# Output projection of a two-layer trunk by seven half-size products, on one core

## The chip, the core and the metric

One core of a Trainium2 chip runs the whole program as one launch. The metric is the device time of the launch in microseconds (us), the median of the runs. The engines are PE (TensorE), DVE (VectorE), ACT (ScalarE), POOL (GpSimd) and SP (SyncE), which in this kernel only issues DMA transfers. Each engine works through its own queue in order and waits at an instruction until the semaphores that it names are there, so an instruction that waits holds up everything behind it on its engine.

## The reference

Two layers with D = 1024 channels and T = 1024 positions, then one RMSNorm. Each layer, cut to what matters here:

```
h = rmsnorm(x) * (1 + scale) + shift
p = h @ w_in                      # q, k, v and gates of 8 heads, 256 wide each
heads 0-3: y = sigmoid(o) * layernorm(mlstm(q, k, v)) * silu(z)
heads 4-7: y = layernorm(retention(rotary(q), rotary(k), v)) * silu(z)
x = x + gate * (concat(y) @ w_out)   # (1024 x 2048) @ (2048 x 1024)
```

The change concerns the last line. Everything is f32.

## The kernel before, in words

**Arithmetic on PE.** An f32 factor is split in two rounded parts, H (a cast, on ACT) and L (the value minus H, a subtraction on POOL or DVE; `split_to`, L589 to L591). `mm3` (L134 to L136) then makes each f32 product of three matmuls, H by H, H by L and L by H, summed in PSUM. The usual matmul has 128 rows and 512 columns. In the profile, a cast is the line L590, a POOL or DVE subtraction L591, and `b`, `wH`, `wL`, `raw`, `g`, `th`, `acc` are tags of SBUF buffers (62, 6, 6, 4, 6, 5 and 4 of them); a tag's buffer comes free when its last reader is done. `pp` and `pa` are four PSUM banks each.

**Order.** PE's queue is written by hand: the main line runs a generator of "units" of 12 matmuls of 512 columns (`run_units`), and after each unit `tick` lets the generators that were started with `launch` do a step, so that attention, norms and loads lie between the units of a projection. ACT, DVE, POOL and SP are ordered by a scheduler from the program's data flow, except in the first stretch, which is written out. All DMA transfers go through SP's queue.

**A head.** For each of the eight heads, `gate_path` makes the gates g (stored to DRAM as `gdr`, L523), then q, k and v come with their own projections, k's rows through DRAM (`kdr`: stored by L622, loaded by `k_rows`, L632, scaled by ACT at L646 and split by DVE at L648), and `launch(attention(...))` puts the head's attention beside the projections of the next head. Its norm is a chain over engines: DVE statistics (L808, L809), DVE `va` (L824), POOL power (L825), DVE `nmu` (L827), ACT `n` (L830); the result goes to DRAM as `ndr` (L842).

**Output projection.** `out_units` runs four passes, 2 halves of 512 positions by 2 halves of 512 output channels (cc). Each pass goes over k = 16 pieces of 128 inner channels, and each piece is 4 tiles of 128 positions by one `mm3`: 2 x 2 x 16 x 4 x 3 = 768 matmuls of 128x512 in a layer. `OutLoads.stage` prepares a piece: it loads a 128x512 block of w_out and splits it (L590 on ACT, L591 on DVE for cc = 0 and on POOL for cc = 1); for cc = 0 it also loads `ndr` and `gdr`, multiplies them (L882, DVE), casts the product times the norm's gain (L885, ACT) and makes the low part (L886, DVE, a product and a subtraction in one). The split y is kept in `b` for cc = 1. After the 16 pieces `out_evac` multiplies each bank by the adaLN gate (L927), adds the residual (L928) and squares it for the next norm (L931). At the end of layer 0 `norm_later` normalizes, transposes on PE (L296) and splits h for layer 1 (L1076 and about); `first` starts the gates' projections from it while the second half is made. At the very end `final_rows` does the closing norm tile by tile.

Of the kernel before, what the change touches and what calls it, by code (L numbers as in the profile page):

```python
# [11 lines left out]
F32 = mybir.dt.float32  # L12
# [57 lines left out]
def tile_hybrid_trunk(ctx, tc, x, c, positions, w_ada, b_ada, norm_g, w_in, conv_w, conv_b,  # L70
# [62 lines left out]
    def mm3(o, lt, rt, start, stop):  # L133
        PE.matmul(o, lt[0], rt[0], start=start, stop=False)  # L134
        PE.matmul(o, lt[0], rt[1], start=False, stop=False)  # L135
        PE.matmul(o, lt[1], rt[0], start=False, stop=stop)  # L136
# [21 lines left out]
    mdr = [dpool.tile([NH, T], F32, name=f"mdr{l}") for l in range(DEPTH)]  # L158

# [552 lines left out]
    def attention(l, hg, gt, qT, kT, kt, vs, gp, rot):  # L712
# [120 lines left out]
        def finish(j):  # L833
# [10 lines left out]
            if hg == 3 and j == NCH - 1:  # L844
                with tc.issue_after(last.ins):
                    load_rotary(rot)

# [17 lines left out]
    class OutLoads:  # L865
        def __init__(self, l):
            self.l, self.yT, self.ready = l, [None] * 16, []
            self.todo = [(half, cc, k) for half in range(2) for cc in range(2) for k in range(16)]

        def stage(self, n=1):  # L870
            for half, cc, k in self.todo[:n]:
                raw = wt("raw", 512, 4)
                Q.dma_start(raw, w_out[self.l, k * P:(k + 1) * P, cc * 512:(cc + 1) * 512])
                wH, wL = wt("wH", 512, 6, F32R), wt("wL", 512, 6, F32R)
                split_to((wH, wL), raw, G if cc else V)
                if cc == 0:
                    hg, ct = k // 2, k % 2
                    yr, gr = wt("g", 512, 6), wt("g", 512, 6)
                    Q.dma_start(yr, ndr[self.l][hg][half].rearrange("b j t -> (b j) t")[ct * P:(ct + 1) * P])
                    Q.dma_start(gr, gdr[self.l][hg][ct][half])  # L880
                    g4 = gr.rearrange("p (a b c) -> p a b c", a=4, c=32)
                    V.tensor_tensor(g4, yr.rearrange("p (b a c) -> p a b c", a=4, c=32), g4, ALU.mult)  # L882
                    y2 = (bt(F32R), bt(F32R))
                    gn = gn_col(self.l, hg, ct)
                    A.activation(y2[0], gr, AF.Copy, scale=gn)  # L885
                    V.scalar_tensor_tensor(y2[1], gr, gn, f(y2[0]), ALU.mult, ALU.subtract)  # L886
                    self.yT[k] = y2
                self.ready.append((self.yT[k], (wH, wL)))
            del self.todo[:n]
# [5 lines left out]
    def out_units(l, half, cc, loads, gb, xnew, ss, done=None):  # L895
        banks = [ps_a() if cc else ps_p() for _ in range(4)]

        def product(k, piece, tt):
            (yH, yL), w = piece
            ts = slice(tt * P, (tt + 1) * P)  # L900
            mm3(banks[tt], (yH[:, ts], yL[:, ts]), w, k == 0, k == 15)

        together = 12 if done else 16
        for k in range(together):
            piece = loads.take()
            for tt in range(4):
                product(k, piece, tt)
            yield
        if not done:
            out_evac(l, half, cc, banks, gb, xnew, ss, range(4))  # L910
        else:
            pieces = [loads.take() for _ in range(together, 16)]
            for tt in range(4):
                for k in range(together, 16):
                    product(k, pieces[k - together], tt)
                out_evac(l, half, cc, banks, gb, xnew, ss, (tt,))
                done((tt,))
                yield

    def out_evac(l, half, cc, banks, gb, xnew, ss, rows):  # L920
        for tt in rows:
            row = half * 4 + tt
            xr = bt()
            srcx = x[row * P:(row + 1) * P] if l == 0 else xdr[row]
            Q.dma_start(xr, srcx[:, cc * 512:(cc + 1) * 512])
            tmp = wt("th", 512, 5)
            V.tensor_tensor(tmp, banks[tt], gb[cc], ALU.mult)  # L927
            V.tensor_tensor(xr, xr, tmp, ALU.add)  # L928
            if l < DEPTH - 1:
                Q.dma_start(xdr[row][:, cc * 512:(cc + 1) * 512], xr)  # L930
            A.activation(tmp, xr, AF.Square, accum_out=ss[:, tt, cc:cc + 1])  # L931
            xnew[tt][cc] = xr
# [13 lines left out]
    def norm_later(l, xt, ss, hT, half):  # L946
        sst = row_rstd(ss, "nrm")
        norm_scale(xt, sst)
# [14 lines left out]
    def final_rows(xn, ss, half, fg, rows):  # L963
        sst = row_rstd(ss, "nrm", rows)
        for tt in rows:
            V.tensor_tensor(xn[tt][1], xn[tt][1], fg[1], ALU.mult)
# [12 lines left out]
    def gains_later(xn, fg):  # L979
        for tt in range(4):  # L980
            yield 2
            V.tensor_tensor(xn[tt][0], xn[tt][0], fg[0], ALU.mult)
# [58 lines left out]
    for l in range(DEPTH):  # L1041
# [85 lines left out]
        for hg in range(8):  # L1127
# [3 lines left out]
            if hg > 0:  # L1131
                gp = [[None, None], [None, None]]
                run_units(gate_path(l, hg, hT, gp, 0, 1 if hg == 7 else 2))
# [16 lines left out]
            if hg == 7:  # L1150
                loads = OutLoads(l)
# [3 lines left out]
            if hg == 1 and l == 0:  # L1155
                launch(rotary_tables(), 0)
            if hg == 5:
# [3 lines left out]
        nhT = [[None, None] for _ in range(KT)]  # L1161
        if l == DEPTH - 1:
            fg = []
# [4 lines left out]
        for half in range(2):  # L1168
# [43 lines left out]
```

## Time and profile before

| what | value |
|---|---|
| median of 3 runs | 2354.23 us (2353.19 to 2355.81) |
| profiled execution: its span, from its first to its last instruction | 2353.8 us, granted clock 0.994 |
| PE busy | 2307.7 us (98%), 12597 matmuls recorded |
| DVE, ACT, POOL busy | 1289.8, 893.3 and 882.8 us (55, 38 and 38%) |
| DMA | 260.50 MB, 111 GB/s over the span |
| output projection of layer 0 | about 1016 to 1205 us |
| output projection of layer 1 | about 2160 to 2344 us, then the closing norm until 2353.8 |

The profiled execution's own time stands beside the median as 2353.8 to 2354.23 us. Busy PE is the union of matmuls that overlap in the pipeline: one 128x512 matmul is recorded with some 0.39 us, while the next starts 0.23 us later, so what a matmul costs is read from start to start.

### The profile page before, as it was taken

What the parts mean: (1) busy time and instruction counts of PE and PEld (TensorE: products, weight loads), DVE (VectorE), ACT (ScalarE), POOL (GpSimd) and SP (SyncE); (2) the same over time, 40 slices, a digit from 0 to 9 for tenths busy, and PEclk for the clock granted to TensorE, in tenths of its full rate; (3) what the DMA queues carried; (4) which work ended last, traced back from release to release, by engine and by line L of the source; (5) the groups of instructions that cost most, each with busy time, mean ns of one, the idle gap of its engine ahead of it and who ended that gap; (6) DMA issues with size and microseconds to landing.
All of it is one profiled execution on the core that took longest, in us unless ns stands there. A gap on an engine that the chain in (4) does not pass through costs nothing.

```text
span 2353.8 us, 34446 instructions
## 1 busy us (share of the span) xinstructions
PE 2307.7 (98%) x12597; PEld 1982.2 (84%) x12597; DVE 1289.8 (55%) x2699; ACT 893.3 (38%) x1736; POOL 882.8 (38%) x841
## 2 busy tenths in 40 slices
PE   5999999999999999999999999999999999999998
PEld 4888888988978988988888888888898888888886
DVE  7375687656454445475525655454543444555753
ACT  5535443444332322343434444344443322224442
POOL 0344333443244343323453444343334434341313
PEclk8999999999999999999999999999999999999999
DMA  7223232434332433277422333322323242425762
GB/s 243 74 68 99 73 88 72 116 94 126 108 99 71 117 83 102 81 241 254 167 78 77 82 76 78 80 68 76 81 70 86 77 112 77 117 82 159 266 231 77
DMA packets 326971, 260.50 MB, mean 111 GB/s; under 512 B 75893, under 2 KB 262013, under 8 KB 326801
## 3 DMA queue, kind: packets, MB, share of 16 engines
q1 hardware_dynamic: 326800, 258.30, 37.4%
q8 instruction: 99, 1.62, 0.3%
q14 instruction: 72, 0.58, 0.1%
HBM read 202.61 MB, written 55.61 MB: 110 GB/s over the span
## 4 chain that ended last, share of the span: by engine, by line
PE 93%; DVE 2%; DMA 2%; issue 1%; POOL 1%; ACT 1%; SPq 1%; POOLq 0%; ACTq 0%; DVEq 0%
PE pp L134 24%; PE pp L136 24%; PE pp L135 24%; PE pa L136 6%; PE pa L134 6%; PE pa L135 6%; PE pa L742 1%; DMA b<-in_w_ada_dram 1%; DMA b<-in_x_dram 1%; PE pa L296 0%; DVE b L233 0%; DMA dm<-mdr 0%; POOL wL L591 0%; SPq L995 0%; POOL b L591 0%
## 5 line engine op out<-in xcount | busy, mean ns | idle before, releaser
L134 PE MATMUL pp<-b,wH 128*128 128x512 f32 x1792 | 712.7, 398 | 1.1 <-ACT b L1073 1.1
L135 PE MATMUL pp<-b,wH 128*128 128x512 f32 x1792 | 708.2, 395 | 1.3 <-DVE b L1076 1.3
L136 PE MATMUL pp<-b,wL 128*128 128x512 f32 x1792 | 708.2, 395 | 0.0
L591 POOL TENSOR_TENSOR wL<-raw,wH 128x512 fp32r<-128x512 f32 x338 | 449.2, 1336 | 578.5 <-ACT wH L590 506.5
L136 PEld LDWEIGHTS pp<-b,wL 128*128 128x128 f32 x1792 | 337.8, 189 | 81.0
L134 PEld LDWEIGHTS pp<-b,wH 128*128 128x128 f32 x1792 | 338.7, 189 | 74.1 <-issue 1.5
L135 PEld LDWEIGHTS pp<-b,wH 128*128 128x128 f32 x1792 | 338.4, 189 | 73.7 <-DVE b L1076 2.0
L590 ACT CAST wH<-raw 128x512 fp32r<-128x512 f32 x402 | 247.3, 617 | 390.4 <-PE pp L135 138.3
L136 PE MATMUL pp<-wH,b 128*128 128x256 f32 (+1 forms) x1152 | 353.0, 306 | 1.2 <-DVE b L886 1.1
L134 PE MATMUL pp<-wH,b 128*128 128x256 f32 (+1 forms) x1152 | 353.6, 307 | 0.0
L135 PE MATMUL pp<-wL,b 128*128 128x256 f32 (+1 forms) x1152 | 352.6, 306 | 0.0
L591 POOL TENSOR_TENSOR b<-acc,b 128x256 fp32r<-128x256 f32 (+1 forms) x208 | 200.4, 983 | 319.9 <-ACT b L590 306.0
L136 PEld LDWEIGHTS pp<-wH,b 128*128 128x128 f32 x1152 | 217.2, 189 | 13.5 <-DVE b L886 2.0
L134 PEld LDWEIGHTS pp<-wH,b 128*128 128x128 f32 x1152 | 216.9, 188 | 10.7
L135 PEld LDWEIGHTS pp<-wL,b 128*128 128x128 f32 x1152 | 216.6, 188 | 10.6
L590 ACT CAST b<-acc 128x256 fp32r<-128x256 f32 (+1 forms) x208 | 93.6, 487 | 201.5 <-DVE acc L685 136.5
L608 DVE SCALAR_TENSOR_TENSOR acc<-pp,cols,acc 128x511 f32<-128x511 f32 (+2 forms) x192 | 142.7, 743 | 44.2 <-ACT acc L603 42.0
L591 POOL TENSOR_TENSOR sL<-th,sH 128x384 fp32r<-128x384 f32 x64 | 69.5, 1086 | 155.4 <-ACT sH L590 141.2
L134 PE MATMUL pa<-wH,b 128*128 128x512 f32 x256 | 101.1, 395 | 0.0
L135 PE MATMUL pa<-wL,b 128*128 128x512 f32 x256 | 100.9, 394 | 0.0
L136 PE MATMUL pa<-wH,b 128*128 128x512 f32 x256 | 100.7, 393 | 0.0
L612 ACT ACTIVATE th<-acc 128x512 f32<-128x512 f32 x64 | 40.4, 632 | 146.6 <-DVE acc L610 79.8
(237 smaller groups left out, 3470.9 us busy)
## 6 DMA issues: line engine op xcount, KB each, us to landing
raw<-in_w_in_dram SPq DMA_DIRECT2D x274, 256.0 KB
raw<-in_w_out_dram SPq DMA_DIRECT2D x128, 256.0 KB
b<-in_w_ada_dram SPq DMA_DIRECT2D x96, 256.0 KB
gdr<-g SPq DMA_DIRECT2D x64, 256.0 KB
ndr<-zt SPq DMA_DIRECT2D x128, 128.0 KB
g<-ndr SPq DMA_DIRECT2D x64, 256.0 KB
g<-gdr SPq DMA_DIRECT2D x64, 256.0 KB
acc<-kdr SPq DMA_DIRECT2D x192, 64.0 KB
```

The source lines that it names most:

```text
L134: PE.matmul(o, lt[0], rt[0], start=start, stop=False)
L135: PE.matmul(o, lt[0], rt[1], start=False, stop=False)
L136: PE.matmul(o, lt[1], rt[0], start=False, stop=stop)
L590: A.copy(dst[0], src)
L591: eng.tensor_tensor(dst[1], src, f(dst[0]), ALU.subtract)
L608: V.scalar_tensor_tensor(acc[:, d:], pt[:, 0:HALF - d], wcol, acc[:, d:], ALU.mult, ALU.add)
L612: A.activation(th, acc, AF.Tanh, scale=0.5)
L742: PE.matmul(pd, kk[i][:, jo + P:jo + CH], qd, start=dt == 0 and i == 0, stop=dt == 1 and i == 1)
```

## The change

**Seven products instead of eight.** The layer's product is Y (1024 x 2048) times W (2048 x 1024). Both are cut into quarters (positions x inner channels, inner x output channels), and the four result quarters come from seven products of quarters in Strassen's scheme (Winograd's form), in the order 1, 2, 5, 6, 3, 7, 4. Each product has 8 pieces of 12 matmuls: 7 x 8 x 12 = 672 matmuls in a layer. PE's row count goes from 12511 to 12319.

- Products 1 and 2 take quarters of Y and W as they are, product 3 a sum of Y's quarters and a quarter of W, products 5, 6 and 7 sums of W's quarters, with sums of Y's quarters (5, 6) or a quarter (7), and product 4 a quarter of Y and a sum of W's. The sums of Y are made on DVE in `OutPrep.stage` (`add`, L939 after the change), the split of y and of sums on ACT and DVE (L595, L596), all splits of weights on POOL.
- Four times in a layer a product is added to a bank that must first be saved or used: after product 1 the banks are copied to `acc` by ACT (L1037), after 5 to buffers of other tags (L1037), after 6 to `g` (L1053, and added to the first copy on DVE, L1054), after 7 to `th`.
- `bases` adds the copies, times the gate, to the residual rows ahead of the last products (L1005, L1006).
- Each product ends with its last 2 pieces in the order of the tiles (the very last product with 4).

**What runs earlier.** `weight_sums`, launched after head 3, loads the 32 blocks of w_out in a layer, makes 32 differences on DVE (L894) and stores them to DRAM (`tdr`). `gated_later`, launched as each half of heads 0 to 6 is normalized, loads `ndr` and `gdr`, multiplies (DVE), scales by the gain (ACT) and stores the gated output to DRAM (`ydr`): 28 of them in a layer, 256 KB each. The output projection loads `ydr` and `tdr`. Head 7 is gated inside the output projection, as all heads were before.

**Head 7.** Both units of its gate path come after q, k and v, beside its attention; before, one of them came first.

**Norm at the layer's end.** The eight scalings alternate between DVE and ACT.

**Scheduler.** It is told to order by its own simulated timeline (`schedule_with_timeline_sim=True`). So ACT, DVE, POOL and SP have another order in many places of the whole body, except in the hand-written start.

The diff, cut to its core (lines in [] are shortened):

```diff
+    def gated(l, hg, ct, half, out=None):
+        yr, gr = wt("g", 512, 6), wt("g", 512, 6)
+        Q.dma_start(yr, ndr[l][hg][half].rearrange("b j t -> (b j) t")[ct * P:(ct + 1) * P])
+        Q.dma_start(gr, gdr[l][hg][ct][half])
...
+        V.tensor_tensor(o4, yr.rearrange("p (b a c) -> p a b c", a=4, c=32), g4, ALU.mult)
+        A.activation(out, out, AF.Copy, scale=gn_col(l, hg, ct))
+    def gated_later(l, hg, half):
+        for ct in range(2):
+            Q.dma_start(ydr[l][2 * hg + ct][half], gated(l, hg, ct, half))
+            yield 2
+    def weight_sums(l):
...
+        for i in range(KT):
+            w11, w12 = load(i, 0), load(i, 1)
+            yield 2
+            difference(w11, w12, w11, 1, i)
...
+        ORDER = (1, 2, 5, 6, 3, 7, 4)
         def stage(self, n=1):
+            for p, i in self.todo[:n]:
+                if p == 1:
+                    self.y11[i] = src = self.y(i, 0)
+                elif p == 2:
+                    self.y12[i] = src = self.y(8 + i, 0)
+                    self.y21[i] = self.y(i, 1)
+                elif p == 5:
+                    self.y22[i] = self.y(8 + i, 1)
+                    src = self.add(V, self.y21[i], self.y21[i], self.y22[i], ALU.add)
+                elif p == 6:
+                    self.s2[i] = src = self.add(V, bt(), self.y22[i], self.y11[i], sub)
+                elif p == 3:
+                    src = self.add(V, self.y12[i], self.y12[i], self.s2[i], sub)
+                else:
+                    src = self.y11[i] if p == 7 else self.y22[i]
+                y2 = self.split_y(src, V)
+                if p == 2:
+                    self.add(V, self.y11[i], self.y11[i], self.y21[i], sub)
...
+    def out_projection(l, prep, gb, fg, nhT):
+        def save(banks, res, place):
+            def evac(tt):
+                res[tt] = wt("acc", 512, 4) if place is None else spare(place + tt)
+                A.copy(res[tt], banks[tt])
...
+        run_units(out_units(prep, b1, True, False, save(b1, c1, None)))
...
+        run_units(out_units(prep, b2, True, False, save(b2, c5, 0)))
...
-                run_units(gate_path(l, hg, hT, gp, 0, 1 if hg == 7 else 2))
+                if hg < 7:
+                    run_units(gate_path(l, hg, hT, gp))
...
-    with tile.TileContext(nc) as tc:
+    with tile.TileContext(nc, schedule_with_timeline_sim=True) as tc:
```

**Three places in the order.** The names are tags with a number for the use.

First, ACT at the start of head 4's attention in layer 0. L830 (L835 after the change) is the norm `n` of the attention, L646 (L651) scales head 4's k rows. Before:

```order
522 L830 ACTIVATE n_7337<-pa_7314,nmu_7335,rsd_7332 128x256
523 L830 ACTIVATE n_7337<-pa_7318,nmu_7335,rsd_7332 128x256
524 L590 CAST wH_7702<-raw_7700 128x512
525 L518 ACTIVATE th_7352<-pp_7301 128x512
526 L646 ACTIVATE b_7200<-acc_7142 128x512
527 L646 ACTIVATE b_7205<-acc_7147 128x512
```

and after:

```order
535 L651 ACTIVATE b_7496<-acc_7436 128x512
536 L523 ACT_TABLE_LOAD
537 L523 ACTIVATE th_7571<-pp_7523 128x512
538 L651 ACTIVATE b_7501<-acc_7441 128x512
539 L595 CAST wH_8023<-raw_8021 128x512
540 L651 ACTIVATE b_7577<-acc_7506 128x512
541 L595 CAST sH_7597<-th_7593 128x384
542 L595 CAST wH_8029<-raw_8027 128x512
543 L523 ACTIVATE th_7656<-pp_7601 128x512
544 L835 ACTIVATE n_7641<-pa_7618,nmu_7639,rsd_7636 128x256
545 L835 ACTIVATE n_7641<-pa_7622,nmu_7639,rsd_7636 128x256
```

The k rows' scalings moved from behind the norm to ahead of it.

Second, DVE inside the output projection of layer 0. Before, two input pieces of the first pass (L882 gates, L886 low part of y, L591 low part of the weights):

```order
1307 L591 TENSOR_TENSOR wL_11016<-raw_11013,wH_11015 128x512
1308 L882 TENSOR_TENSOR g_11020<-g_11019,g_11020 128x512
1309 L882 TENSOR_TENSOR g_11085<-g_11084,g_11085 128x512
1310 L886 SCALAR_TENSOR_TENSOR b_11025<-g_11020,cols_388,b_11024 128x512
1311 L886 SCALAR_TENSOR_TENSOR b_11090<-g_11085,cols_388,b_11089 128x512
1312 L591 TENSOR_TENSOR wL_11081<-raw_11078,wH_11080 128x512
```

and after, two pieces of product 6, each with the subtraction that makes its y, the one that makes product 3's y from it, and the split's (L596):

```order
1386 L939 TENSOR_TENSOR b_11818<-b_11584,b_10902 128x512
1387 L939 TENSOR_TENSOR b_11297<-b_11297,b_11818 128x512
1388 L596 TENSOR_TENSOR b_11821<-b_11818,b_11820 128x512
1389 L939 TENSOR_TENSOR b_11842<-b_11609,b_10914 128x512
1390 L939 TENSOR_TENSOR b_11326<-b_11326,b_11842 128x512
1391 L596 TENSOR_TENSOR b_11845<-b_11842,b_11844 128x512
```

DVE's weight splits and gate products of the projection are gone from here, and sums of y stand there, every one with both inputs in SBUF.

Third, ACT inside the output projection. Before, its casts of weights (L590), the scaled cast of y (L885) and, between them, casts of the next layer's h (`b<-acc`):

```order
791 L885 ACTIVATE b_11817<-g_11813,cols_388 128x512
792 L590 CAST wH_11922<-raw_11920 128x512
793 L590 CAST b_11840<-acc_11838 128x512
794 L885 ACTIVATE b_11855<-g_11851,cols_388 128x512
795 L590 CAST wH_11960<-raw_11958 128x512
```

and after, where product 5 ends and product 6 begins on the same banks (`pa`):

```order
796 L595 CAST wH_11906<-raw_11904 128x512
797 L1037 COPY cf_11872<-pa_11679 128x512
798 L595 CAST b_11844<-b_11842 128x512
799 L1037 COPY n_11880<-pa_11680 128x512
800 L1037 COPY kw_11888<-pa_11681 128x512
801 L595 CAST b_11856<-b_11854 128x512
802 L595 CAST wH_11932<-raw_11930 128x512
803 L1037 COPY zt_11896<-pa_11682 128x512
```

The four copies stand between the casts of pieces that product 6 needs.

230 lines of the change are left out of this document (153 added, 77 removed).

## The prediction

> **What bounds the kernel now.** I read the windows by stage first, since the change takes work from one stage and puts work into the others (the two long rows are the heads of layers 0 and 1, the row behind each is that layer's output projection, the last row the closing norm).
>
> ```profile
> core 0: us, PE busy (x) PEld busy (x) DVE busy (x) ACT busy (x) POOL busy (x), PEclk, DMA share, GB/s
> 80.00:1010.00 930.00, 922.65 (x5231) 801.31 (x5230) 532.78 (x1185) 341.84 (x668) 363.33 (x346) 1.00 0.33 92
> 1010.00:1203.00 193.00, 191.86 (x897) 157.57 (x896) 105.62 (x161) 75.14 (x135) 70.88 (x53) 1.00 0.63 209
> 1220.00:2150.00 930.00, 929.26 (x5269) 807.98 (x5266) 473.15 (x1041) 348.44 (x686) 372.64 (x368) 1.00 0.31 82
> 2150.00:2345.00 195.00, 193.99 (x893) 159.03 (x891) 113.27 (x180) 76.66 (x141) 55.43 (x44) 1.00 0.60 203
> 2345.00:2354.00 9.00, 0.00 (x0) 0.00 (x0) 2.87 (x8) 2.06 (x4) 1.39 (x2) 0.69 0.38 145
> ```
>
> PE is busy for 99% or more of each stage but the last, at a granted clock (PEclk) of 1.00. Beside PE's own weight loads no engine is busy for more than 59% of any. So the time is the number of matmuls times their price from start to start. That price I took from PE's timeline, which has 40 matmuls of 128x512 without a gap from the first to the last of these rows:
>
> ```profile
> 1202.50 0.39 PE L136 MATMUL pa<-wH,b 128*128 128x512 f32 x1
> ...
> 1211.57 0.39 PE L136 MATMUL pp<-b,wL 128*128 128x512 f32 x1
> ```
>
> That is 39 steps in 9.07 us, 0.2326 us each; the 0.39 us are one matmul's own length in the pipeline. A piece of 12 matmuls takes 2.79 us.
>
> Then PE's waits, and the rows of its timeline at those that the change moves:
>
> ```profile
> PE pa L184 <- DMA rows<-in_b_ada_dram: 7.5, 1, 7.5
> PE pa L207 <- DMA rows<-in_c_dram: 2.9, 1, 2.9
> PE pa L134 <- ACT b L646: 2.7, 1, 2.7
> ```
>
> ```profile
> 689.61 0.58 PE L134 MATMUL pa<-b,b 128*128 128x256 f32 x1 [2.74 <-ACT b L646]
> 1017.44 0.50 PE L136 MATMUL pp<-wH,b 128*128 128x512 f32 x1 [1.14 <-DVE b L886]
> 1212.40 0.33 PE L296 MATMUL pa<-ident,b 128*128 128x128 f32 x1 [0.22 <-DVE b L291]
> 1213.19 0.33 PE L296 MATMUL pa<-ident,b 128*128 128x128 f32 x1 [0.46 <-DVE b L291]
> ```
>
> The two waits on DMA are in the start, which stays as it is. After it no DMA holds PE.
>
> **The change, part by part.**
>
> *Matmuls.* 768 - 672 = 96 fewer in a layer, 192 in all, every one 128x512: 192 x 0.2326 = 44.7 us, all on the path, since PE is the bound. The Trainium skill (TensorE: Matmul & The Clock Gate, "Wait — 56ns, not 53.3ns?") gives 215.7 ns from start to start for 512 columns in a warm array; by that the saving would be an estimated 41.4 us. The row here says 0.2326, and the sum goes by the row.
>
> *Waits that go.* At 689 us PE waits for L646 on ACT. ACT's and DVE's timelines show why:
>
> ```profile
> 684.82 1.19 DVE L824 TENSOR_TENSOR va<-mv,kc 128x2 f32<-128x2 f32 x1
> 687.02 1.02 ACT L830 ACTIVATE n<-pa,nmu,rsd 128x256 f32<-128x256 f32 x2 [2.86 <-DVE nmu L827]
> 687.93 0.61 ACT L590 CAST wH<-raw 128x512 fp32r<-128x512 f32 x1
> 688.44 0.60 ACT L518 ACTIVATE th<-pp 128x512 f32<-128x512 f32 x1
> 688.93 1.15 ACT L646 ACTIVATE b<-acc 128x512 fp32r<-128x512 f32 x2
> ```
>
> L646 stands in ACT's queue behind the attention's norm L830, which waits 2.86 us for DVE and POOL. In the new order the k rows' scalings stand nine and six rows ahead of that norm, so they run as soon as their loads land: -2.74 us. At 1017 us PE's first output piece waits for the low part of its y (L886), which goes through load, product, cast and low part in the projection itself; now the first product's y is gated long before and only split here: -1.14. At the layer boundary the last 2 pieces go tile by tile, so three tiles are evacuated before the last matmul, and the norm's chain begins earlier: -0.68. Together -4.6 us.
>
> *The tail.* The last 12 matmuls of a tile and the closing chain are of the same kinds as before; 0.
>
> *Bank copies.* Eight times (four in a layer) the next product adds to banks that ACT must first have copied. The copy itself isn't in the trace of before; its nearest row is an ACT operation of the same shape that reads PSUM, and beside it the cast that can stand ahead of it:
>
> ```profile
> L603 ACT ACTIVATE acc<-pp,cols 128x512 f32<-128x512 f32 x64 | 49.5, 773 | 23.7 <-PE pp L136 23.6
> L590 ACT CAST wH<-raw 128x512 fp32r<-128x512 f32 x402 | 247.3, 617 | 390.4 <-PE pp L135 138.3 <-PE pp L136 136.9 <-PE pa L136 58.0
> ```
>
> The last bank's product ends, and nine matmuls (tiles 0 to 2 of the next piece) lie before its reuse: 9 x 0.2326 = 2.09 us. One cast and the copy take 0.62 + 0.77 = 1.39, two casts and the copy 2.01: hidden, by 0.08 us at the least. If ACT's front cast waits for DVE (1.25 us, the stretched row below) with another cast behind it, the wait is 2.01 + 1.25 - 2.09 = 1.17 us. Ends 0 and 8 x 1.17 = 9.4 us; the copies are issued among casts that mostly have their data, so nearer the lower end, a quarter: +2.4.
>
> *DVE and POOL in the output projection.* Here lies the danger. DVE's and POOL's timelines, from before's projection:
>
> ```profile
> 1033.41 0.74 DVE L886 SCALAR_TENSOR_TENSOR b<-g,cols,b 128x512 fp32r<-128x512 f32 x1
> ...
> 1034.94 0.68 DVE L882 TENSOR_TENSOR g<-g,g 128x512 f32<-128x512 f32 x1
> 1035.54 0.68 DVE L591 TENSOR_TENSOR wL<-raw,wH 128x512 fp32r<-128x512 f32 x1
> 1036.41 1.25 DVE L886 SCALAR_TENSOR_TENSOR b<-g,cols,b 128x512 fp32r<-128x512 f32 x1 [0.19 <-ACT b L885]
> ```
>
> ```profile
> 1034.98 2.13 POOL L591 TENSOR_TENSOR sL<-th,sH 128x384 fp32r<-128x384 f32 x1 [3.91 <-ACT sH L590]
> ```
>
> POOL's subtraction has no overlap elsewhere and takes 1.03 us, and the 128x512 one 1.30:
>
> ```profile
> 683.72 1.02 POOL L591 TENSOR_TENSOR sL<-th,sH 128x384 fp32r<-128x384 f32 x1 [3.14 <-ACT sH L590]
> 684.70 1.30 POOL L591 TENSOR_TENSOR wL<-raw,wH 128x512 fp32r<-128x512 f32 x1
> ```
>
> Here POOL took 2.13 us and ended (1037.11) 0.89 after DVE's second operation (1036.22); the DVE operation that started meanwhile took 1.25 instead of 0.74 and ended (1037.66) 0.55 after POOL. So with both inputs in SBUF the two take turns: after a change of hands an operation costs the other's end plus 0.89 of 1.02 (0.13 less) or 0.55 of 0.74. In a row, DVE's start every 0.60 us. Per layer I count for 56 pieces: 60 POOL subtractions (56 weight splits, 4 in `bases`) and 140 two-input DVE operations (56 splits of y, 32 sums, 4 gate products, 24 in `bases`, 4 in `sum_up`, 20 in `out_rows`). With turns: 60 x (1.30 - 0.13) + 60 x 0.55 + 80 x 0.60 = 151 us. PE needs 56 x 2.79 = 156 us. That is 97%, and it just fits. With DVE's 0.60 throughout and POOL's 1.30 it is 162, with the full 0.68 173. Ends for a layer: 0 and 17 us; I take the row with turns, since these operations do alternate there, and 1 us a layer for a queue that is so full: +2.
>
> The Trainium skill (SBUF — State Buffer, "Who interferes with whom") states that GpSimd has DVE's second port pair, that a DVE instruction with two SBUF inputs contends with a GpSimd one that reads SBUF, and that the one that issues first has the pair for its whole instruction while the other "fully blocks". The rows agree that they block each other, with ends 0.55 and 0.89 us after the other's. By whole durations the sum would come out at the upper end, +17 us a layer: that is the first rival.
>
> *Layer 0's norm in product 7.* The first half's norm now has a whole product's time, but its 9 DVE operations run in that full queue. Ends: 0, and 9 x (1.25 - 0.68) = 5.1 us; most of it lies beside product 7's units, so +1.
>
> *Gated outputs and weight sums in the heads.* Per layer 28 gate products and 32 subtractions on DVE and 28 scalings on ACT come into the heads' stage. From the groups of before:
>
> ```profile
> L882 DVE TENSOR_TENSOR g<-g,g 128x512 f32<-128x512 f32 x64 | 61.6, 968 | 32.7 <-DMA g<-gdr 32.4 <-issue 0.2
> L885 ACT ACTIVATE b<-g,cols 128x512 fp32r<-128x512 f32 x64 | 45.8, 723 | 67.7 <-DVE g L882 67.6
> ```
>
> DVE goes from 533 to 533 + 60 x 0.97 = 591 of 930 us, ACT from 342 to 362: covered by idle time. Transfers: 56 loads, 28 stores, 32 loads and 32 stores of 0.262 MB are 39 MB, 42 GB/s on top of 92 at a share of 0.33, so about 0.48: covered. The stores wait for their data at the head of SP's queue, and weight loads stand behind them. What such a wait costs, SP's timeline shows:
>
> ```profile
> 682.13 7.98 SPq L523 DMA_DIRECT2D gdr<-g  x2
> 690.29 1.84 SPq L632 DMA_DIRECT2D acc<-kdr  x4
> 692.17 1.00 SPq L317 DMA_DIRECT2D raw<-in_w_in_dram  x2
> ```
>
> SP stood for 8 us and nothing of PE waited for the loads behind: 0 as long as the loads are that early.
>
> *The new order everywhere.* In the heads PE idled 930 - 922.65 = 7.35 us in layer 0 and 0.74 in layer 1. The order of four engines is another now. Ends: all of the rest gone, -(7.35 - 2.74 + 0.74) = -5.3; or layer 1 as bad as layer 0, +6.6. Nothing excludes either; added work speaks for the upper one: +2.5.
>
> Sum: 2353.8 - 44.7 - 4.6 + 2.4 + 2 + 1 + 2.5 = 2312.4 us for the profiled execution. The median of the runs is 0.4 above its span, so 2312.8; I say 2312.
>
> **The rivals.**
>
> *The shared lane becomes the bound* (the upper end above, 6 to 17 us a layer, so +12 to +34): about 2322 to 2344. For it: the 97%, no room in products 2, 5, 6 and 3 (two DVE operations and a split a piece, 1.30 + 1.36 = 2.66 of 2.79). Against it: product 1, 7 and 4 are lighter (1.98 a piece), and six weight buffers let the splits run ahead.
>
> *The order also removes the old waits*: layer 0's heads run like layer 1's, and the new costs are hidden: 2353.8 - 44.7 - 4.6 - (7.35 - 2.74 - 0.74) = 2300.6. For it: layer 1 shows that this body can run with 0.74. Against: layer 0 has the rotary tables and layer 1's adaLN columns besides.
>
> *Slower than before*: the same lane, if each operation pays its stretched time without the other gaining. Place: products 2, 5, 6 and 3, 64 pieces in two layers. It decides from 2.79 + 49.3 / 64 = 3.56 us a piece. With DVE at 1.25 twice and POOL at 2.13 a piece takes 4.63, 64 x 1.84 = 118 us more: 2422. Against it: the stretched times hold the other's turn, so the same time is counted twice.
>
> *The matmuls don't go*: PE's row count does fall by 192, so no.
>
> **How the numbers follow.** Forecast (2304 to 2320) 0.65; lane as bound 0.18; old waits gone too 0.11; slower 0.04; 0.02 for a sum of small losses between. A measurement of this kernel can tell 0.2%, 4.7 us, from no change. Only the slower case and a little of the last reach past 2349.5: faster 0.94, same 0.02, slower 0.04. The range goes down to 2300 for the third case and up to 2332, the middle of the second; it leaves out half of the second (0.09), some of the third (0.04) and the slower case: 0.17.
>
> **What would show it.** PE's busy time should fall by about 44 us, with a price of 0.233 kept. PE's wait list should lose L646's 2.7 and L886's 1.1. In the projection's windows DVE and POOL together should be busy for most of the time, DVE operations with two SBUF inputs recorded above 0.9 us on average, and PE's waits there be on the copies (L1037) or on splits (L596): up to some 6 us. I am wrong if PE idles more than 10 us in a projection, if the heads' idle time grows by more than 7 us, or if PE waits on DMA.

## The result: slower by half a percent, and where the saved matmuls went

The changed kernel takes 2368.19 us (median of 4 runs, 2365.19 to 2372.46) against 2355.02 us before: ratio 1.0056, 95% interval 1.0044 to 1.0068. The forecast was 2312 (2300 to 2332). The profiled execution, the slowest of the four, spans 2370.7 us.

The head of its page, and PE's waits of over 2 us in all that are not in the start. The prediction had named the copies (L1037) and the splits (L596) among them:

```profile
span 2370.7 us, 34813 instructions
PE 2283.6 (96%) x12405; PEld 1952.7 (82%) x12405; DVE 1449.7 (61%) x2859; ACT 962.9 (41%) x1872; POOL 1001.5 (42%) x897
```

```profile
PE pa L135 <- POOL wL L596: 8.9, 2, 5.5
...
PE pp L134 <- ACT th L1012: 7.4, 4, 3.6
PE pa L134 <- ACT b L595: 7.1, 3, 3.3
PE pa L134 <- ACT nd L793: 6.5, 4, 3.4
PE pp L135 <- POOL b L596: 5.1, 5, 3.2
PE pp L134 <- ACT acc L1037: 4.6, 3, 2.5
...
PE pa L134 <- ACT n L835: 2.9, 2, 2.6
PE pa L136 <- DVE b L596: 2.1, 1, 2.1
```

The span grew by 16.9 us. PE's idle time (span less busy) went from 2353.8 - 2307.7 = 46.1 to 87.1 us, so 41.0 more. PE's busy time fell by 24.1 where 192 matmuls at 0.2326 are 44.7: the other 20.6 us are matmuls that took longer and are recorded as busy. Some 12 us of them are 62 more steps of 0.43 us instead of 0.23 (shown in the last section); most of the rest are other steps behind waits that came out longer than usual. 41.0 + 20.6 - 44.7 = 16.9. The windows by stage (heads and projection of layer 0, then of layer 1) say where:

```profile
core 0: us, PE busy (x) PEld busy (x) DVE busy (x) ACT busy (x) POOL busy (x), PEclk, DMA share, GB/s
80.00:1012.00 932.00, 922.01 (x5226) 801.89 (x5225) 574.16 (x1245) 360.83 (x699) 377.86 (x353) 0.99 0.46 134
1012.00:1215.00 203.00, 186.63 (x826) 147.85 (x825) 149.95 (x195) 94.29 (x182) 115.85 (x76) 0.97 0.50 155
1215.00:2160.00 945.00, 943.47 (x5362) 819.88 (x5361) 523.62 (x1115) 376.45 (x732) 391.10 (x378) 1.00 0.44 124
2160.00:2356.00 196.00, 174.68 (x732) 138.04 (x731) 144.38 (x187) 83.11 (x161) 100.61 (x62) 0.92 0.44 139
```

The heads, which took in the gated outputs, the sums of weights and 120 stores, lost little (10.0 and 1.5 us idle, before 7.4 and 0.7), and DMA at a share of 0.44 to 0.50 is the releaser of no wait of PE after the start. The two projections lost 16.4 and 21.3 us of idle PE, where they had lost about 2 in all, and their PEclk is down to 0.97 and 0.92. More than 10 us of idle PE in a projection was one of the prediction's signs of being wrong. Summed over PE's timeline, the time beyond each matmul's usual pitch is about 60 us in the two projections (before 3), and in the heads 5 to 7 us more than before.

Inside layer 1's projection, in the stretches of products 6, 3 and most of 7, and then of the end:

```profile
2260.00:2325.00 65.00, 58.88 (x243) 46.44 (x242) 57.48 (x69) 28.10 (x56) 44.87 (x22) 0.95 0.38 118
2325.00:2356.00 31.00, 23.78 (x84) 17.78 (x83) 18.78 (x25) 11.60 (x25) 10.94 (x8) 0.78 0.27 94
```

In 65 us DVE is recorded busy for 57.5 and POOL for 44.9, together 102: each record holds the wait for the other. There was no time at which neither was at work, but for 0.3 us, as the overlap of their rows shows. A stretch of DVE's and of POOL's timeline in it shows the price:

```profile
2295.83 10.04 DVE L596 TENSOR_TENSOR b<-b,b 128x512 fp32r<-128x512 f32 x6 [6.31 <-ACT b L595]
```

```profile
2296.78 8.54 POOL L596 TENSOR_TENSOR wL<-raw,wH 128x512 fp32r<-128x512 f32 x5
```

Six DVE operations in 10.04 us and five POOL operations in 8.54, 1.7 us for each pair: in this stretch they take strict turns, and a DVE operation that costs 0.60 alone costs 1.7. Elsewhere POOL was kept out altogether (its operations of 10 and 13 us, below).

### The profile page after: what moved, and what is told of

It reads as the page before. It is cut to its first block, busy times and chain, and to the rows that moved or that the text cites. A ratio compares the mean times of both kernels' runs of the same rounds, so it can differ in the third digit from the quotient of the medians.

```text
span 2370.7 us, 34813 instructions
## 1 busy us (share of the span) xinstructions
PE 2283.6 (96%) x12405; PEld 1952.7 (82%) x12405; DVE 1449.7 (61%) x2859; ACT 962.9 (41%) x1872; POOL 1001.5 (42%) x897
## 4 chain that ended last, share of the span: by engine, by line
PE 76%; DMA 7%; DVE 6%; issue 4%; ACT 3%; POOL 3%; SPq 2%; POOLq 0%; ACTq 0%; DVEq 0%
PE pp L134 21%; PE pp L135 21%; PE pp L136 21%; PE pa L134 4%; PE pa L135 4%; PE pa L136 3%; DMA b<-ydr 2%; POOL wL L596 1%; PE pa L747 1%; DVE b L939 1%; DMA b<-in_w_ada_dram 1%; ACT b L595 1%; DMA ndr<-zt 1%; DVE b L596 1%; POOL b L596 1%
## 5 line engine op out<-in xcount | busy, mean ns | idle before, releaser
L596 POOL TENSOR_TENSOR wL<-raw,wH 128x512 fp32r<-128x512 f32 x382 | 524.4, 1381 | 548.6 <-ACT wH L595 468.3
L134 PE MATMUL pp<-wH,b 128*128 128x256 f32 (+1 forms) x1136 | 350.1, 308 | 12.1 <-ACT th L1012 7.4
L136 PE MATMUL pp<-wH,b 128*128 128x256 f32 (+1 forms) x1136 | 348.1, 306 | 0.1
L595 ACT CAST wH<-raw 128x512 fp32r<-128x512 f32 x382 | 234.2, 617 | 260.6 <-PE pp L135 168.5
L596 POOL TENSOR_TENSOR b<-acc,b 128x256 fp32r<-128x256 f32 (+1 forms) x208 | 210.2, 1028 | 264.6 <-ACT b L595 264.6
L595 ACT CAST b<-acc 128x256 fp32r<-128x256 f32 (+1 forms) x208 | 94.5, 486 | 151.6 <-DVE acc L690 111.2
L596 DVE TENSOR_TENSOR b<-b,b 128x512 fp32r<-128x512 f32 x112 | 96.7, 877 | 49.8 <-ACT b L595 49.2
L596 POOL TENSOR_TENSOR sL<-th,sH 128x384 fp32r<-128x384 f32 x64 | 67.4, 1052 | 116.9 <-ACT sH L595 111.9
L134 PE MATMUL pa<-b,b 128*128 128x256 f32 (+1 forms) x320 | 92.2, 288 | 9.4 <-ACT nd L793 6.5
L595 ACT CAST b<-b 128x512 fp32r<-128x512 f32 x112 | 67.4, 621 | 80.2 <-DVE b L939 43.9
L596 POOL TENSOR_TENSOR cL<-cf,cH 128x516 fp32r<-128x516 f32 (+1 forms) x48 | 64.4, 1342 | 72.6 <-ACT cH L595 72.6
```

Source lines behind the costliest of these rows:

```text
L134: PE.matmul(o, lt[0], rt[0], start=start, stop=False, skip_group_check=more)
L136: PE.matmul(o, lt[1], rt[0], start=False, stop=stop, skip_group_check=more)
L595: A.copy(dst[0], src)
L596: eng.tensor_tensor(dst[1], src, f(dst[0]), ALU.subtract)
```

## The experiments

Two theories went into the runs. *Lane*: DVE operations with two SBUF inputs and POOL's operations use one lane, and in the projections it is full. *Order*: the new order of ACT, SP and POOL puts waiting instructions ahead of urgent ones.

**The order taken back.** Without the timeline ordering, all else as changed:

```diff
-    with tile.TileContext(nc, schedule_with_timeline_sim=True) as tc:
+    with tile.TileContext(nc) as tc:
```

> The change as it is, but without the scheduler's timeline ordering. Two theories. Lane: DVE and POOL block each other at SBUF in the output projections; the order is not the cause. Then the projections still lose some 40 to 70 us of PE idle and slow-clock time and the run stays between 2355 and 2380 us. Order: the new order puts waiting instructions ahead of urgent ones on ACT, SP and POOL. Then this run gets at least half of the 58 us back and lies at 2340 us or below.

Measured 2397.60 us, ratio to before 1.0179 (1.0163 to 1.0194). Both theories had it at 2380 or less. Taken as a whole the order is no cause of the loss; it is worth 29 us in the changed kernel. PE's list of waits shows what for:

```profile
PE pa L134 <- ACT b L595: 18.5, 10, 3.3
PE pp L134 <- ACT th L1012: 9.9, 4, 5.9
```

**The order alone**, on the kernel before:

```diff
-    with tile.TileContext(nc) as tc:
+    with tile.TileContext(nc, schedule_with_timeline_sim=True) as tc:
```

> The kernel before with the timeline ordering alone. Lane: within 6 us of before (2349 to 2361), since nothing is added to the projections; the heads of layer 0 may lose the 4 us that they lost in the changed kernel. Order: 10 us or more slower than before (2365 and up).

Measured 2346.57 us, ratio 0.9966 (0.9953 to 0.9979): 8.5 us faster, better than either theory said. So against what the ordering alone gives, the seven products and their feed cost 21.6 us.

**Four subtractions moved from POOL to DVE.** In the changed kernel the first subtraction of `bases` (L1024) took 10.07 us in layer 0 and 13.08 in layer 1, with weight splits behind it on POOL, and PE waited 3.4 and 5.5 us for those:

```profile
2277.56 13.08 POOL L1024 TENSOR_TENSOR g<-g,cf 128x512 f32<-128x512 f32 x1 [4.24 <-DMA b<-xdr]
2290.61 3.73 POOL L596 TENSOR_TENSOR wL<-raw,wH 128x512 fp32r<-128x512 f32 x3
```

```profile
2291.92 0.79 PE L135 MATMUL pa<-wL,b 128*128 128x512 f32 x1 [5.52 <-POOL wL L596]
```

```diff
-                    G.tensor_tensor(plus[tt], plus[tt], less[tt], ALU.subtract)
+                    V.tensor_tensor(plus[tt], plus[tt], less[tt], ALU.subtract)
```

> The change with the four subtractions a layer in bases (line 1024) on DVE instead of POOL; the weight splits stay on POOL. Lane: the two subtractions that took 10.07 and 13.08 us are no longer ahead of weight splits on POOL, so the stalls behind them (3.4 and 5.5 us, and some 2 us of slow clock each) shrink: about 2355 to 2362 us; the other stalls stay. Order: no change beyond 4 us, since a split in the same place would starve the same way.

Measured 2359.74 us, ratio 1.0021 (1.0011 to 1.0030): 8.4 us less than the changed kernel, as Lane said. But in layer 1 a weight split, the first of the two in this row, now took 13.12 us at nearly the same place, as the other theory had said; only layer 0 lost its long operation.

```profile
2279.21 14.81 POOL L596 TENSOR_TENSOR wL<-raw,wH 128x512 fp32r<-128x512 f32 x2 [4.21 <-ACT wH L595]
```

**No weight split on POOL.**

```diff
-            split_to(w2, raw, G)
+            split_to(w2, raw, V)
```

together with the edit before, so that POOL takes no part in the products' feed.

> The change with all weight splits of the output projection and the four subtractions on DVE, none on POOL. A layer's projection then has some 200 DVE operations with two SBUF inputs at 0.60 us, 120 us of 156. Lane: nothing blocks DVE any more, and the projections lose at most 20 us in both layers instead of 58: 2315 to 2335 us. Order: DVE has more to do in the same kind of order, so 2360 us or more.

Measured 2322.18 us, ratio 0.9857 (0.9840 to 0.9873): 46.0 us less than the changed kernel, though DVE has 60 operations more in a layer. This decides for Lane. The windows of its two projections:

```profile
1010.00:1200.00 190.00, 184.32 (x840) 148.80 (x839) 153.62 (x250) 97.52 (x185) 28.76 (x20) 0.99 0.52 164
2125.00:2312.00 187.00, 183.28 (x832) 148.47 (x830) 150.87 (x266) 92.69 (x179) 10.39 (x11) 0.99 0.50 162
```

DVE does 250 instructions in 154 us, where the changed kernel's did 195 in 150; PE idles 5.7 and 3.7 us, and 13 steps at the lower clock are left in them, of 60 in the changed kernel. The weight splits' group shows what one costs with POOL out of the way (mean 684 ns, against 1452 ns on POOL in the changed kernel's projection of layer 0):

```profile
L596 DVE TENSOR_TENSOR wL<-raw,wH 128x512 fp32r<-128x512 f32 x49 | 33.3, 684 | 5.8 <-ACT wH L595 5.7
```

**Another operand on POOL.** Is it POOL beside DVE, or only that POOL was too slow for the weights? The run before, with the split of y on POOL and that of the weights on DVE:

```diff
-                y2 = self.split_y(src, V)
+                y2 = self.split_y(src, G)
```

> The run without POOL splits, but with the split of y on POOL instead of DVE: the same 56 POOL subtractions in a layer as the changed kernel has, another operand. Lane: 56 POOL operations beside some 140 on DVE again, so the gain of the run without POOL splits is lost: 2350 to 2380 us. Rival, that only the weights' path was too slow on POOL (cast, then 1.3 us, with six buffers): the y path has its own buffers and is ahead, so 2320 to 2335 us.

Measured 2363.49 us, ratio 1.0035 (1.0020 to 1.0050). 41 of the 46 us are lost again, with the weights off POOL. So it is POOL's splits beside DVE's work that cost, whichever path they belong to. The mean of POOL's splits was 1583 ns here.

**Half of them.**

```diff
-            split_to(w2, raw, V)
+            split_to(w2, raw, V if i % 2 else G)
```

(`i` is the piece's number in its product, which the edit hands down to this line.)

> The run without POOL splits, but every second piece's weight split on POOL (28 in a layer). Lane by time: a POOL operation holds 1.17 us, so 60 x 0.60 less for DVE and 28 x 1.17 more on the lane makes 28 x 1.17 + 172 x 0.60 = 136 us of 156: it fits, and the run is within 8 us of 2322. Lane by starving: POOL gets in only where DVE pauses, and each POOL split can wait for a whole run of DVE operations: 2330 to 2350 us.

Measured 2339.67 us, ratio 0.9932 (0.9913 to 0.9951): 17.5 us more than with none. The sum of times, 136 of 156 us, said it would fit; it did not. The second case, that POOL gets in only where DVE pauses, had 2330 to 2350, and the trace shows it in both layers: a POOL split (the first of the two in the row below) took 16.11 us while DVE went on with an operation every 0.60 us, and PE waited 5.5 and 5.6 us for these two splits:

```profile
PE pa L135 <- POOL wL L596: 11.1, 2, 5.6
```

```profile
2255.79 17.34 POOL L596 TENSOR_TENSOR wL<-raw,wH 128x512 fp32r<-128x512 f32 x2 [7.42 <-ACT wH L595]
```

**Where, not how many.** POOL splits in products 1, 2 and 5 only, 24 in a layer:

```diff
-            split_to(w2, raw, V)
+            split_to(w2, raw, G if light else V)
```

(`light` is true for products 1, 2 and 5; the edit hands it down.)

> The run without POOL splits, but with the weight splits of products 1, 2 and 5 on POOL (24 in a layer, against 28 in the run with every second one). In the changed kernel either DVE or POOL was busy for 82 of 95 us in those three products, and for 84 of 84 in products 6 and 3 and the beginning of 7. If the loss comes from where the lane is full, and not from the count of POOL operations: 2320 to 2328 us. If it goes by the count: 24 / 28 of the 17 us that the other run lost, 2335 to 2339.

Measured 2322.36 us, ratio 0.9853 (0.9836 to 0.9869), the same as with none. So 24 POOL splits in the first three products cost nothing, and 28 spread over all cost 17.5 us: the place counts. PE's timeline shows which. A product has 96 matmuls, 22.3 us without a wait; from the first start of one product to that of the next it took, in us for layer 0 and layer 1:

| run | product 5 | 6 | 3 | 7 |
|---|---|---|---|---|
| the changed kernel | 28.2, 31.9 | 23.1, 23.2 | 29.6, 30.2 | 25.3, 24.9 |
| no POOL splits | 23.4, 28.0 | 22.3, 22.2 | 22.2, 22.3 | 25.8, 22.3 |
| every second one | 22.6, 31.8 | 23.3, 22.7 | 30.7, 30.9 | 24.0, 22.2 |
| in products 1, 2 and 5 only | 26.1, 28.7 | 22.3, 22.3 | 22.3, 22.3 | 23.9, 22.4 |

Product 3 is the main place; in the changed kernel product 5 took 4 to 5 us longer too than without POOL splits, and in the last product of layer 1 PE waited 7.2 us for copies (L1012). In the changed kernel the lane is full in product 3: DVE started 28 and 30 operations of 128x512 and POOL 11, and at the prediction's prices that is an estimated 28 x 0.60 + 11 x 1.17 = 29.7 and 30.9 us; it took 29.6 and 30.2. In 5, 6 and 3 each piece needs a sum and a split on DVE (in 7 only the split), and from product 6 on `bases` and `sum_up` (L1005, L1006, L1054) come on top. In the run with every second split the same sum for product 3 is only 34 x 0.60 + 4 x 1.17 = 25.1 us in layer 0 and, with 39 operations on DVE, 28.1 in layer 1, yet it took 30.7 and 30.9: there the long POOL operation adds to it, and product 3 alone holds 17 of the 17.5 us. That product 1's free time can't be used, since pieces are prepared only three ahead, is argued and not shown.

**The order, without POOL.**

```diff
-    with tile.TileContext(nc, schedule_with_timeline_sim=True) as tc:
+    with tile.TileContext(nc) as tc:
```

> The run without POOL splits, and without the timeline ordering. Lane: the ordering is worth what it is worth in the kernel before (8.5 us) and a little in the projections: 2330 to 2342 us. Order as a cause of its own: as with POOL splits, where it was worth 29 us: 2348 us or more.

Measured 2342.93 us, ratio 0.9952 (0.9936 to 0.9968). The ordering is worth 20.8 us here, 29 with POOL splits and 8.5 in the kernel before. In the two kernels with seven products nearly all of it lies in product 5, the one that gates head 7's output: without the ordering it took 33.2 and 37.7 us here (23.4 and 28.0 with it), and 37.4 and 49.8 with POOL splits (28.2 and 31.9). The time is below the second case and just above the first.

**Head 7's gates as before**, one unit ahead of q, k and v:

```diff
-                if hg < 7:
-                    run_units(gate_path(l, hg, hT, gp))
+                run_units(gate_path(l, hg, hT, gp, 0, 1 if hg == 7 else 2))
...
-                run_units(gate_path(l, hg, hT, gp, 0, 1))
```

> The run without POOL splits, with one unit of head 7's gate path back in front of q, k and v, as before the change. Attention of head 7 then reaches further into products 1 and 2, and head 7's output, which product 5 gates, is ready later. If that is worth something: 2326 to 2335 us; if the order of head 7 is a cause of the loss: below 2319; else within 3 us of 2322.

Measured 2336.72 us, ratio 0.9924 (0.9908 to 0.9941): 14.5 us more. This part of the change is a gain, and I had given it no term at all.

**What is left in the projections.** Two edits on the run without POOL splits: five pieces prepared ahead instead of three, and the norm's gain put on the loaded rows, ahead of the product with the gates.

```diff
-                loads.stage(1)
+                loads.stage(3)
```

> The run without POOL splits, with five pieces of the output projection prepared ahead instead of three. If what is left of the loss in the projections (some 10 us) comes from pieces that are prepared too late: 2314 to 2319 us. If it comes from queues that are ordered badly in places: within 4 us of 2322.

```diff
-        V.tensor_tensor(o4, yr.rearrange("p (b a c) -> p a b c", a=4, c=32), g4, ALU.mult)
-        A.activation(out, out, AF.Copy, scale=gn_col(l, hg, ct))
+        A.activation(yr, yr, AF.Copy, scale=gn_col(l, hg, ct))
+        V.tensor_tensor(o4, yr.rearrange("p (b a c) -> p a b c", a=4, c=32), g4, ALU.mult)
```

> The run without POOL splits, with the gain of the head's norm put on the loaded rows (ACT), ahead of the product with the gates (DVE), instead of behind it: head 7's pieces in product 5 then have DVE to DVE behind the product, one change of engine less after the last load. 2317 to 2321 us if head 7's chain is what PE waits for at the end of product 5 (2.2 and 0.6 us); else within 3 us of 2322.

2318.97 us, ratio 0.9850 (0.9836 to 0.9865), and 2317.33 us, ratio 0.9844 (0.9828 to 0.9861). Each is 3 to 5 us below 2322.18, near what its runs differ among themselves (2317.54 to 2321.99 and 2315.13 to 2320.98). The first time fits both of its cases, the second the case of head 7's chain. But in PE's timeline product 5 took 23.4 and 28.4 us in the first and 22.2 and 28.4 in the second, against 23.4 and 28.0 without the edits, so the gains are hardly at product 5's end, and that the times fit is partly luck. Both together:

> The run without POOL splits with both of the last edits: five pieces prepared ahead and the gain on the loaded rows. Each brought 3 to 5 us where PE waited for pieces at product 5's end. If they take away different waits: 2312 to 2316 us; if the same: 2316 to 2319.

2317.00 us, ratio 0.9829 (0.9810 to 0.9849), 2311.07 to 2320.90. They don't add up clearly, and the run with the gain alone is as fast. This is 38 us, 1.7%, below before.

**The lane by itself.** Probes behind the end of the run without POOL splits, which take no part in the result: DVE runs of N operations of 128x512, and one POOL subtraction beside them, each probe waiting for the one before.

```diff
+        V.tensor_tensor(s, src, src2, ALU.add)
+        for kind in kinds:
+            if kind == "two":
+                V.tensor_tensor(t, s, fg[0], ALU.add)
+            elif kind == "psum":
+                V.tensor_tensor(t, bank, s, ALU.add)
...
+        G.tensor_tensor(u, s, fg[0], ALU.subtract)
```

> The run without POOL splits, and after its end six probes, one behind the other, that take no part in the result: DVE makes one sum, then a run of N operations of 128x512 without a pause, and one POOL subtraction of 128x512 starts when the first sum is there. Runs: 4, 8 and 16 operations with both inputs in SBUF; 16 with one input in PSUM; 16 in turns of two of each kind; none. If the two take turns, POOL's operation takes some 1.9 us (1.3 and one DVE operation) whatever N is. If POOL gets in only where DVE's two-input run ends, it takes about 0.6 N + 1.2 us: 3.6, 6.0 and 10.8. With one input in PSUM and with none about 1.3; in turns of two and two about 2.5, as it gets in at the first PSUM operation.

POOL's six operations, for runs of 4, 8 and 16 with two SBUF inputs, 16 with one input in PSUM, turns of two and two, and none:

```profile
2317.69 1.76 POOL L1337 TENSOR_TENSOR g<-acc,b 128x512 f32<-128x512 f32 x1 [1.56 <-DVE acc L1329]
2322.34 1.76 POOL L1337 TENSOR_TENSOR g<-acc,b 128x512 f32<-128x512 f32 x1 [2.88 <-DVE acc L1329]
2329.88 1.77 POOL L1337 TENSOR_TENSOR g<-acc,b 128x512 f32<-128x512 f32 x1 [5.78 <-DVE acc L1329]
2343.22 1.26 POOL L1337 TENSOR_TENSOR g<-acc,b 128x512 f32<-128x512 f32 x1 [11.58 <-DVE acc L1329]
2355.62 1.77 POOL L1337 TENSOR_TENSOR g<-acc,b 128x512 f32<-128x512 f32 x1 [11.13 <-DVE acc L1329]
2368.96 1.26 POOL L1337 TENSOR_TENSOR g<-acc,b 128x512 f32<-128x512 f32 x1 [11.57 <-DVE acc L1329]
```

With an input in PSUM POOL takes 1.26 us, its time alone (as with no run). With two SBUF inputs it takes 1.76 or 1.77 whatever N is, and 1.77 in turns of two and two: it waits for one DVE operation, then has its turn. So the first case, turns, held, and the operations of 10 and 13 us are not explained by it. Three more probes looked for what made those: independent targets instead of one, POOL arriving in the middle of a run, and DVE operations that each wait for ACT.

> The six probes again, with other runs of DVE. In the first probes each DVE operation wrote the tile of the one before it, so they came at 0.72 us and POOL took 1.76 us whatever the run's length; in the projections, where POOL took 10 to 16 us, DVE's operations were independent and came at 0.60, each before the end of the last. Here the runs write different tiles: 4, 8 and 16 two-input operations; then 16 that write one tile; 16 with one input in PSUM; and three times four two-input operations and one with PSUM. If overlap is what keeps POOL out: about 0.6 N + 1.2 us for the first three (3.6, 6.0, 10.8), 1.8 for the fourth, 1.3 for the fifth, and the last one 3.6, as it gets in at the first PSUM operation, or the whole 10 us. If POOL always gets in after one operation: 1.8 in all but the fifth.

> The probes once more, with POOL's operation arriving in the middle of DVE's run: it reads the result of the run's fourth operation. Behind those four come 4, 8 and 16 independent two-input operations (0.60 us apart), 16 that write one tile (0.72 apart), 16 with one input in PSUM, and three times four two-input ones and one with PSUM. In the projections POOL's long operations (10 to 16 us) began while such a run was under way, and ended 1.1 us after it; in the earlier probes POOL's operation began together with the run's first and got in behind it. If it is the arrival in the middle that matters: 0.6 N + 1.1 us for the first three (3.5, 5.9, 10.7), about 1.8 for the fourth, 1.3 for the fifth; the sixth shows whether one PSUM operation lets POOL in (3.5) or not (10). If POOL gets in after one operation there too: 1.8 in all but the fifth, and what held it up in the projections stays open.

> Four probes behind the end as before, with POOL's operation arriving in the middle of DVE's run (behind its fourth operation). First 16 independent operations without a wait, as before; then 16 of which each waits for its own input from ACT, which ACT has made shortly before; the same with the rounded output type of the splits; the last one with 8. If a wait that each DVE operation carries is what keeps POOL out, as in the projections: 1.6 us for the first, 10.7 for the second and third, 5.9 for the last. Else 1.6 to 1.8 in all, and it stays open.

POOL took 1.77 us in the first of the three whatever the length, and 1.64 to 1.67 us in the other two, but for runs with PSUM inputs (1.26 or 1.27). DVE's runs show the other side, here for 4, 8 and 16 independent operations of the first of the three:

```profile
2317.14 3.56 DVE L1333 TENSOR_TENSOR b<-b,acc 128x512 f32<-128x512 f32 x4
...
2321.53 5.97 DVE L1333 TENSOR_TENSOR b<-b,acc 128x512 f32<-128x512 f32 x8
...
2328.33 10.79 DVE L1333 TENSOR_TENSOR b<-b,acc 128x512 f32<-128x512 f32 x16
```

(10.79 - 5.97) / 8 = 0.60 us an operation, and 3.56 - 4 x 0.60 - 0.08 = 1.08 us that DVE lost to the one POOL operation. All three expectations named a cause for the long ones, and none held. What kept POOL out for 10 to 16 us in five places (two in the changed kernel, one in the run with the subtractions on DVE, two in the run with every second split; all in product 3, and each ended 1.1 us behind a run of DVE) stays open. No probe had more than one POOL operation in a run. In the run of the changed kernel without the timeline ordering, with the same work on POOL, none of these operations took over 3.6 us, so POOL's share of the work alone does not make them. How much of the 46 us they cost stays open too: moving the subtractions brought 8 and left one of them in place, and with every second split they stand where nearly the whole loss is.

## Why the prediction was wrong, point by point

- *Matmuls, -44.7.* Right in number and price: 192 fewer, at 0.233 outside the stalls. But "PE's busy time should fall by about 44" was wrong, 24.1, since I had left out that matmuls behind a long wait can run slower and count as busy (below).
- *Waits that go, -4.6.* The scalings of head 4's k rows (L651) are no longer waited for, but PE waits a little later, at 699.0 us, for the norm behind them: `ACT n L835`, 2.6 us. The 1.14 at the first piece went. At the layer's boundary new and longer waits took the place of 0.68 (`POOL b L596`, 3.2 us). So the three places together cost about 1 us more than before, and did not gain 4.6.
- *Bank copies, +2.4, at most 9.4.* PE waited 13.9 us for them (L1012 7.4, L1037 4.6, L1053 1.9). The upper end took one cast waiting 1.25 us for DVE. What stood ahead was worse: ACT's casts wait for loads, and loads for SP, which is in order too. At the end of layer 1 this is how it reads on ACT:

```profile
2336.34 0.62 ACT L595 CAST b<-raw 128x512 fp32r<-128x512 f32 x1 [2.98 <-DMA raw<-tdr]
2336.86 0.61 ACT L595 CAST wH<-raw 128x512 fp32r<-128x512 f32 x1
...
2338.01 0.56 ACT L1012 COPY th<-pp 128x512 f32<-128x512 f32 x1
```

and on SP, where eight stores of the finished half stood ahead of that load:

```profile
2326.97 0.34 SPq L1109 DMA_DIRECT2D out_dram<-b  x1
...
2330.85 0.60 SPq L1109 DMA_DIRECT2D out_dram<-b  x1
2331.56 2.00 SPq L928 DMA_DIRECT2D raw<-tdr  x3
```

  With the splits off POOL these waits are 1.5 us in all, so they came with POOL's splits and not from the copies themselves.
- *DVE and POOL in the output projection, +2.* This is the step that failed. Its price was right where the two take turns: 0.55 + 1.17 = 1.72 us a pair, and the alternation shows 1.7. Wrong was the sum over a whole layer, 151 us against PE's 156, taken as fitting. It left out other work on DVE and POOL in that time (head 7's attention, the next layer's splits, the final gains), and it averaged over seven products where pieces are prepared three ahead. The demand stands in a few of them: at the same prices product 3 needs 29.7 and 30.9 us where PE needs 22.3, and it took that long. Wrong was also that "these operations do alternate there": in three versions POOL was kept out for 10 to 16 us, which had no term at all. The term was 1 us a layer, with 17 at its upper end; the two projections lost about 26 and 35 us, and 46 us in all went with POOL's operations. The runs show that the loss comes from POOL's operations beside DVE's; how it divides between a full lane and POOL kept out stays open.
- *The rule of the Trainium skill* (SBUF — State Buffer, "Who interferes with whom"), that a DVE instruction with two SBUF inputs and a GpSimd one that reads SBUF block each other, holds here, with the numbers above; its whole durations gave the higher of my two sums, and the higher was nearer. The operations of 10 to 16 us, beside which DVE ran more than a dozen of its own, go beyond that rule.
- *The rivals.* The lane as bound (0.18) had the right mechanism and a price of 12 to 34 us; taking POOL's operations off it brought 46. The slower case (0.04) came true in sign by luck: it had each operation pay its stretched time, 118 us, while the turns cost what the forecast had read from the rows.
- *Gated outputs and weight sums in the heads* and *the new order everywhere*: the heads lost some 5 to 7 us more than before, against +2.5 and a gain of 2.74. The order itself is a gain in every pair of runs, 8.5 to 29 us, for which I had only a range around zero.

## What to carry to other kernels

In this kernel an engine at 55% and one at 38% were one full resource in one stretch: where both work on SBUF, add DVE's two-input time and POOL's, per stage and not per layer, with only as much averaging as the buffers allow. Trading matmuls for sums moves work from the engine with the most regular queue to those that share a lane; the sum to make first is the feed of the busiest stretch. Here a subtraction takes 0.68 us on DVE and 1.3 on POOL, and where DVE has two-input work waiting it loses 1.1 us to it, so moving it "to the idle engine" costs DVE more than doing it. In products 1, 2 and 5, where the two engines left time free, it cost nothing that the runs could tell.

## What the runs showed of the hardware that I had not expected

Behind most waits of 2.1 to 5.5 us PE's matmuls came at about half their rate for a while: the rows behind layer 1's longest wait are 0.43 us apart (2.56 us for six steps), then 0.23 again.

```profile
2292.51 0.63 PE L136 MATMUL pa<-wH,b 128*128 128x512 f32 x1
...
2295.07 0.63 PE L136 MATMUL pa<-wH,b 128*128 128x512 f32 x1
2295.49 0.51 PE L134 MATMUL pa<-wH,b 128*128 128x512 f32 x1
2295.84 0.40 PE L135 MATMUL pa<-wL,b 128*128 128x512 f32 x1
```

PE's timeline has 90 such steps (0.42 to 0.44 us between matmuls of 512 columns) in the changed kernel, 28 before (22 of them in the first 80 us) and 42 without POOL splits. Each costs 0.2 us, so such a wait costs one to two microseconds more than it lasts. The granted clock between 2291 and 2297 us is 0.61. The Trainium skill (TensorE: Matmul & The Clock Gate, "What's actually happening") has a gate that halves PE's clock after an idle window of about 3.4 us, and "Wait — 56ns, not 53.3ns?" there gives 426.7 ns from start to start for 512 columns at the halved clock; the 0.427 here agrees. In this trace a wait of 2.51 us (at 2196.5 us, then seven steps of 0.42 to 0.68) was enough, and behind one of 2.55 us (at 699.0 us) the matmuls kept their usual pitch, so the length of the wait alone does not decide.
